# An interleave of two arrays: whole-tile stores in longer rows, three shared load buffers and a shrinking tail

## The chip, the cores and the metric

The kernel runs on one core of a Trainium2 chip. The metric is the device time of one execution in microseconds. The profile is one execution with the hardware profiler on; its span is a little shorter than the device time, since it runs from the first to the last recorded instruction.

## What is computed

Two float32 arrays of 32 x 256 x 1024 (33.55 MB each) are interleaved along the last axis into one of 32 x 256 x 2048:

```python
result = np.zeros((batch, seq, dim * 2), dtype=np.float32)
result[..., 0::2] = x
result[..., 1::2] = y
```

There is no arithmetic. 67.1 MB are read and 67.1 MB are written.

## The kernel before

Since the interleave doesn't care about rows, the kernel treats x, y and out as flat lists: element i of x goes to place 2i, element i of y to place 2i + 1. The lists are cut into 8 pieces of 128 x 8192 elements. In a piece, each of the 128 partitions holds one stretch of 8192 neighbouring elements, so one load moves 128 rows of 32 KB.

One pass of the loop (L50) does this:

- SP issues the load of x (L56) and of y (L57) into `xtile` and `ytile`. Each has its own pool with two buffers of 32 KB per partition.
- VectorE handles the piece in two halves (L60). For each half it copies 4096 columns of x into the even places of `otile` (L70), and 4096 columns of y into the odd places (L71). `otile` comes from a pool with two buffers of 32 KB per partition.
- ACT issues the store of each half (L72): 128 rows of 32 KB.

So there are two queues, one for loads (q1 in the profile, issued by SP) and one for stores (q10, issued by ACT). Each engine issues in the order of the program. A load waits until the copies have read the buffer that it overwrites (two passes ago); the first copy of a half waits until the store that last used its `otile` buffer (two halves ago) has landed; a store waits for both copies.

Ahead of the loop, a store of 16 rows of 512 bytes of zeros goes out on ACT's queue (L47); the first real store overwrites its place in the output. After the program is built, the first load is moved ahead of the opening barrier (L86 to L104), so that it starts early. The change leaves both as they are, but for the distance between the zero rows, which follows the width of a tile.

Of the kernel before, what the change touches and what calls it, by code (L numbers as in the profile page):

```python
# [2 lines left out]

# [4 lines left out]


@with_exitstack
def _interleave(
    ctx: ExitStack,
    tc: tile.TileContext,
    x: bass.AP,
    y: bass.AP,
    out: bass.AP,
):
    nc = tc.nc
    P = 128  # L20

    total = 1
    for s in x.shape:
        total *= s

    WL = 8192
    WS = 4096

    xf = x.rearrange("b s d -> (b s d)")
    yf = y.rearrange("b s d -> (b s d)")  # L30
    of = out.rearrange("b s d -> (b s d)")

    fp32 = mybir.dt.float32

    xpool = ctx.enter_context(tc.tile_pool(name="xp", bufs=2))
    ypool = ctx.enter_context(tc.tile_pool(name="yp", bufs=2))
    opool = ctx.enter_context(tc.tile_pool(name="op", bufs=2))

    lwidths = [WL] * (total // P // WL)
    assert sum(lwidths) == total // P  # L40


    wpool = ctx.enter_context(tc.tile_pool(name="wp", bufs=1))
    zero = wpool.tile([16, 128], fp32, name="zero")
    nc.vector.memset(zero, 0.0)  # L45
    first = dataclasses.replace(of, offset=0, ap=[[2 * WL, 16], [1, 128]])
    nc.scalar.dma_start(out=first, in_=zero)  # L47

    start = 0
    for lw in lwidths:  # L50
        xtile = xpool.tile([P, WL], fp32, name="xtile")[:, :lw]
        ytile = ypool.tile([P, WL], fp32, name="ytile")[:, :lw]

        xs = dataclasses.replace(xf, offset=start, ap=[[lw, P], [1, lw]])
        ys = dataclasses.replace(yf, offset=start, ap=[[lw, P], [1, lw]])
        nc.sync.dma_start(out=xtile, in_=xs)  # L56
        nc.sync.dma_start(out=ytile, in_=ys)  # L57

        soff = 0
        while soff < lw:  # L60
            width = min(WS, lw - soff)
            otile = opool.tile([P, 2 * WS], fp32, name="otile")[:, : 2 * width]
            os_ = dataclasses.replace(
                of,
                offset=2 * start + 2 * soff,
                ap=[[2 * lw, P], [1, 2 * width]],
            )
            xsub = xtile[:, soff : soff + width]
            ysub = ytile[:, soff : soff + width]
            nc.vector.tensor_copy(out=otile[:, 0::2], in_=xsub)  # L70
            nc.vector.tensor_copy(out=otile[:, 1::2], in_=ysub)  # L71
            nc.scalar.dma_start(out=os_, in_=otile)  # L72
            soff += width

        start += P * lw
    assert start == total


def kernel(tc, x, y, out):
    nc = tc.nc  # L80
    _interleave(tc, x, y, out)
    tc.close()
    tc.compile()  # L83


    blocks = nc.main_func.blocks  # L86
    opening = blocks[0].instructions
    at, moved = next(
        (b, i)
        for b in blocks[1:]  # L90
        for i in b.instructions
        if i.engine == mybir.EngineType.SP and i.opcode == "DMACopy"
    )
    assert not moved.sync_info.on_wait
    body = at.instructions
    body.remove(moved)
    gate = next(
        n
        for n, i in enumerate(opening)
        if i.engine == mybir.EngineType.SP and i.opcode == "Drain"  # L100
    )
    opening.insert(gate, moved)
    at.instructions = body
    blocks[0].instructions = opening  # L104


# [1 line left out]
_INS = ['x', 'y']  # L108
_OUTS = [((32, 256, 2048), 'float32')]


# [23 lines left out]
```

## Time and profile before

| | before |
|---|---|
| device time, median of 3 runs | 316.41 us (315.72 to 316.87) |
| span of the profiled execution | 313.8 us |
| VectorE busy | 72.8 us, 23% |
| DMA | 134.23 MB, mean 428 GB/s |
| copies of 128 x 4096 | 32, of 2.29 us each |
| loads | 16, of 4096 KB, rows of 32 KB |
| stores | 16, of 4096 KB, rows of 32 KB |

The page gives the busy time of each engine, the span in 40 slices, and the share of 16 DMA engines that each queue's packets took. A packet is here one row of a transfer, or one completion signal of a few bytes. A transfer of 128 rows gives 8 rows to each of the 16 DMA engines. A transfer has "landed" when all 16 have signalled.

### The profile page before, as it was taken

Reading aid. Unit: us, or ns where it says so; the run is one execution under the profiler, and the core shown is the slowest. Engines: PE = TensorE matmul, PEld = TensorE weight load, DVE = VectorE, ACT = ScalarE, POOL = GpSimd, SP = SyncE. Lnnn points to the kernel's source line nnn. Section 1 sums busy time; section 2 is a strip of 40 time slices with the busy share of each in tenths; the row PEclk is TensorE's granted clock in tenths of the full one; section 3 lists DMA queues with packets and bytes.
Section 4 is the critical chain, followed back from the end, with each engine's and each line's share of the span. In section 5 each row is a group of like instructions: output and inputs, shape, how many; then the busy total and the mean of one; then the engine's idle time right before and its main releaser. Section 6 shows DMA issues by size and latency. Waiting matters only on the chain.

```text
span 313.8 us, 152 instructions
## 1 busy us (share of the span) xinstructions
DVE 72.8 (23%) x33; POOL 0.2 (0%) x4
## 2 busy tenths in 40 slices
DVE  0433002231032410325003150130501305023500
POOL 0000000000000000000000000000000000000000
DMA  8999999999999999999999999999999999999997
GB/s 339 464 405 397 468 401 464 405 464 405 464 405 464 405 459 409 451 418 451 418 434 434 430 439 426 443 413 455 401 468 401 468 401 468 401 468 401 464 405 334
DMA packets 4640, 134.23 MB, mean 428 GB/s; under 512 B 528, under 2 KB 544, under 8 KB 544
## 3 DMA queue, kind: packets, MB, share of 16 engines
q1 hardware_dynamic: 2304, 67.11, 49.9%
q10 hardware_dynamic: 2336, 67.12, 49.5%
HBM read 67.11 MB, written 67.12 MB: 428 GB/s over the span
## 4 chain that ended last, share of the span: by engine, by line
DMA 83%; DVE 11%; DVEq 1%; issue 0%
DMA out_dram<-otile 76%; DMA ytile<-in_y_dram 7%; DVE otile L71 6%; DVE otile L70 5%; DVEq L83 1%; DVEq L70 0%
## 5 line engine op out<-in xcount | busy, mean ns | idle before, releaser
L70 DVE COPY otile<-xtile 128x4096 f32<-128x4096 f32 x16 | 36.6, 2295 | 184.9 <-DMA out_dram<-otile 173.7
L71 DVE COPY otile<-ytile 128x4096 f32<-128x4096 f32 x16 | 36.6, 2292 | 39.8 <-DMA ytile<-in_y_dram 39.8
L45 DVE MEMSET zero<- 16x128 f32 x1 | 0.2, 165 | 0.9 <-PEq L119 0.9
L119 POOL MEMSET const-bfloat16-1.0<- 128x1 bf16 x1 | 0.1, 102 | 0.0
L119 POOL MEMSET const-uint8-127<- 128x1 uint8 x1 | 0.1, 102 | 0.0
L119 POOL MEMSET const-float32-0.0<- 128x1 f32 x1 | 0.1, 99 | 0.2 <-issue 0.2
L119 POOL MEMSET const-float32-1.0<- 128x1 f32 x1 | 0.1, 99 | 0.0
## 6 DMA issues: line engine op xcount, KB each, us to landing
out_dram<-otile ACTq DMA_DIRECT2D x16, 4096.0 KB, 29.1
xtile<-in_x_dram SPq DMA_DIRECT2D x8, 4096.0 KB, 43.6
ytile<-in_y_dram SPq DMA_DIRECT2D x8, 4096.0 KB, 60.7
out_dram<-zero ACTq DMA_DIRECT2D x1, 8.0 KB, 6.3
```

Source lines behind the costliest of these rows:

```text
L45: nc.vector.memset(zero, 0.0)
L70: nc.vector.tensor_copy(out=otile[:, 0::2], in_=xsub)
L71: nc.vector.tensor_copy(out=otile[:, 1::2], in_=ysub)
L83: tc.compile()
L119: nc = _bacc.Bacc("TRN2", target_bir_lowering=False, num_devices=1)
```

## The change

The widths are now a list: eight tiles of 7296 columns (28.5 KiB rows in x and y), then tiles of 4096, 2048 and 1024. Their sum is the same 65536 columns per partition. A tile is no longer stored in halves: VectorE copies the whole of x and the whole of y into an `otile` of twice the width, and one store writes rows of 57 KiB. As this takes more room per `otile` buffer (57 KiB, still two), x and y share one pool of three load buffers instead of two each. The shrinking tiles at the end are there so that the last copies and the last store are short.

```diff
-    WL = 8192
-    WS = 4096
+    WIDTHS = [7296] * 8 + [4096, 2048, 1024]
+    WMAX = max(WIDTHS)
...
-    xpool = ctx.enter_context(tc.tile_pool(name="xp", bufs=2))
-    ypool = ctx.enter_context(tc.tile_pool(name="yp", bufs=2))
+    lpool = ctx.enter_context(tc.tile_pool(name="lp", bufs=3))
     opool = ctx.enter_context(tc.tile_pool(name="op", bufs=2))
...
+    for w in WIDTHS:
+        tiles = []
+        for src in (xf, yf):
+            t = lpool.tile([P, WMAX], fp32, name="ltile")[:, :w]
+            rows = dataclasses.replace(src, offset=start, ap=[[w, P], [1, w]])
+            nc.sync.dma_start(out=t, in_=rows)
+            tiles.append(t)
+        otile = opool.tile([P, 2 * WMAX], fp32, name="otile")[:, : 2 * w]
+        for i, t in enumerate(tiles):
+            nc.vector.tensor_copy(out=otile[:, i::2], in_=t)
+        rows = dataclasses.replace(of, offset=2 * start, ap=[[2 * w, P], [1, 2 * w]])
+        nc.scalar.dma_start(out=rows, in_=otile)
+        start += P * w
```

There are now 22 loads, 22 copies and 11 stores.

More of the change, by code (lines that the diff above doesn't have):

```diff
@@ L24, in _interleave @@
         total *= s
-    WL = 8192
-    WS = 4096
+    assert P * sum(WIDTHS) == total
     xf = x.rearrange("b s d -> (b s d)")
@@ L33, in _interleave @@
     fp32 = mybir.dt.float32
-    xpool = ctx.enter_context(tc.tile_pool(name="xp", bufs=2))
-    ypool = ctx.enter_context(tc.tile_pool(name="yp", bufs=2))
+    wpool = ctx.enter_context(tc.tile_pool(name="wp", bufs=1))
+    lpool = ctx.enter_context(tc.tile_pool(name="lp", bufs=3))
     opool = ctx.enter_context(tc.tile_pool(name="op", bufs=2))
-    lwidths = [WL] * (total // P // WL)
-    assert sum(lwidths) == total // P
-    wpool = ctx.enter_context(tc.tile_pool(name="wp", bufs=1))
     zero = wpool.tile([16, 128], fp32, name="zero")
@@ L45, in _interleave @@
     nc.vector.memset(zero, 0.0)
-    first = dataclasses.replace(of, offset=0, ap=[[2 * WL, 16], [1, 128]])
+    first = dataclasses.replace(of, offset=0, ap=[[2 * WIDTHS[0], 16], [1, 128]])
     nc.scalar.dma_start(out=first, in_=zero)
     start = 0
[L50 to L75, printed above, removed]
@@ L76, in _interleave @@
-    assert start == total
+    for w in WIDTHS:
[11 more added lines that the diff above has]
+        start += P * w
```

## The prediction

> **What bounds the kernel now.** I read the slices of the page first, then the DMA queues, then stretches of the trace, and the waits and the chain last, because the first two already say that one resource is full.
>
> ```profile
> DMA  8999999999999999999999999999999999999997
> ...
> q1 hardware_dynamic: 2304, 67.11, 49.9%
> q10 hardware_dynamic: 2336, 67.12, 49.5%
> ```
>
> The two shares are of 16 engines over 313.8 us, and they add to 99.4%: q1 carries the loads, q10 the stores, and the DMA engines have next to no idle time between the first slice and the last. VectorE, at 23%, cannot be the bound. Each queue moved 2048 rows of 32 KB (16 transfers of 128 rows). A store row takes 0.495 x 16 x 313.8 / 2048 = 1.213 us. A load row averages 1.223 us; by the packet records the excess is in two places, the first row of each engine (1.47 to 2.27 us) and one row of each at 26 to 29 us, as the first big store comes in (1.69 to 1.88 us); all others take 1.21 to 1.23.
>
> Next, stretches of one loop pass each (start:end, length, VectorE busy, GpSimd busy, clock, DMA share, GB/s):
>
> ```profile
> 67.44:106.16 38.72, 9.09 (x4) 0.00 (x0) 1.00 1.00 433
> 106.16:144.89 38.73, 9.09 (x4) 0.00 (x0) 1.00 1.00 433
> 144.89:183.61 38.72, 9.09 (x4) 0.00 (x0) 1.00 1.00 433
> ```
>
> A pass moves 16.78 MB in 38.72 us at DMA share 1.00, and it repeats. Eight passes are 309.8 us of the 313.8. The other 4 us are 0.99 us ahead of the first row, some 1.3 us of slow first rows, and the end (last row ends at 312.70, landing 313.06, span 313.8).
>
> The waits and the chain must be read beside this:
>
> ```profile
> DVE otile L70 <- DMA out_dram<-otile: 173.7, 14, 21.6
> DVE otile L71 <- DMA ytile<-in_y_dram: 39.8, 8, 5.2
> ...
> DMA 83%; DVE 11%; DVEq 1%; issue 0%
> ```
>
> VectorE waits for stores to leave their buffers, and the chain counts 11% of copies between stores. It would be wrong to call these 11% a gain: the stretches above, which hold those copies, have the DMA at 1.00. While one buffer is copied, the other store is still running. The end shows it too:
>
> ```profile
> 293.80 2.30 DVE otile L70
> 296.09 2.20 DVEq L83
> ```
>
> The last pair of copies runs to 298.3 us, but the store before it lands only at 303.4, so the last store goes straight in behind it.
>
> **What the Trainium skill says.** "DMA: Bandwidth & Descriptors", section "Where 436 GB/s comes from", puts the ceiling of the 16 ports at 435.2 GB/s. The trace agrees: 433 in every pass. There is no rate left to win. The same page, "Queues, rings and completion order", says that an engine takes turns between its queues packet by packet. In the trace between 29.1 and 48 us, with both queues full, the rows are shared like this:
>
> ```profile
> q1 hardware_dynamic: 144, 4.19, 51.4%
> q10 hardware_dynamic: 142, 4.13, 50.6%
> ```
>
> That is one row for one row (each count includes 16 completions). Before, where all rows are equal, turns by row and turns by bytes look alike; I take turns by row. "Why small descriptors are slow" states a fixed cost per packet. The trace prices it: the 16 rows of 512 bytes of the zero store took 3.6% of 16 engines in a stretch of 0.75 us, so 27 ns each, against 1213 ns for 32768 bytes. The line through both has 8.2 ns per row and 0.0368 ns per byte.
>
> **The change, part by part.** I call the eight large tiles 0 to 7 and the small ones A (4096), B (2048), C (1024).
>
> *Rows.* Bytes stay. Rows per engine go from 256 to 22 x 8 + 11 x 8 = 264. DMA work: 8 x 8.2 ns = 0.07 us more, 310.6 instead of 310.5. Stores have 40 rows fewer, loads 48 more. A large load row takes 29184 x 0.0368 + 8 = 1.08 us (a transfer 8.65), a large store row 2.15 (17.2). For A, B, C a load takes 4.88, 2.47, 1.27 and a store 9.70, 4.88, 2.47. Assuming that the straight line reaches 57 KB is a choice; it is beyond the sizes seen.
>
> *Copies.* 32 become 22. From 2.29 us for 4096 columns: 4.09 us for 7296, then 2.29, 1.15, 0.57. The elements are the same, so VectorE stays near 73 us in all, hidden as long as the DMA has rows.
>
> *Start.* Three loads instead of four are issued at once. They last 1 + 0.7 + 3 x 8.65 = 27.7 us. The fourth needs only the copy of x of tile 0, over at about 1.7 + 8.65 + 0.4 + 4.1 = 14.9 us. Nothing is lost, and the 0.99 us and the slow rows stay.
>
> *Middle.* A load now waits for the copy of the load three before; SP issues in order, so every later load is queued behind it. A copy of x waits for the store two tiles before. Suppose store t and load y of tile t+1 start together: by row they alternate for 8 x (1.08 + 2.15) = 25.9 us and end together. Then x of t+2 runs alone, 8.65 us; in sum 34.5 us, which is the DMA work of a tile. Meanwhile y of t+1 has to land (0.4 us, as after the last row of all, or up to one store row more), be copied (4.09) and its store has to reach its first row. That last step is unknown: the first load of all took 0.99 us from issue to row, in empty rings; the zero store took 4.2 and the first big store (issued at 24.3) up to 4.8, both behind load rows. So 5.5 to 11.7 us. Loads to move in this time: x of t+2 and, behind it, y of t+2, issued as soon as x of t+1 is copied, over 20 us earlier; 17.3 us together. So no gap. Three load buffers are enough, and the middle costs nothing either way.
>
> *End.* Load rows xA to yC are 48 per engine. Between 9 and 15 are through when store 7 starts; 16 more alternate with the rows of stores 7 and A. So after the last row of A, yB has 1 to 7 rows left, and then only the 16 rows of C, 2.5 us. In this time yB has to land (0.4), be copied (1.15; x of B is copied earlier, its buffer being free since store 7) and store B has to reach its first row (1.0 to 4.6). The DMA stands idle for 2.55 - 2.54 = 0.0 us at the low end, 3.6 at the high end. I take 1.3 for that last step, because the ring has no long rows in it then (a row of C is 0.16 us), and so 0.3 us. Store B lasts 4.88 us, which hides landing and copy of C (0.4 + 0.57). The last landing costs what it did.
>
> Sum: +0.07 + 0.3, so 316.41 + 0.4 = **316.8 us**, no change that can be told.
>
> **Rivals.** *The end is slower.* If the 4.2 to 4.8 us of a store's start are a fixed delay and not load rows ahead of it, B starts 3.6 us late: 316.4 + 0.1 + 3.6 = 320.1 us. For it: both starts on that queue show about the same delay. Against it: in both the engine then had a row of 1.2 to 2.2 us in hand[...], which explains the same. Delays in between give 317.4 to 319. Chance 0.25 in all, 0.08 of it for the full delay.
>
> *Fewer rows in the stores pay.* If store rows over 32 KB cost less than the line says, or the slow first rows are fewer, the most to be had is 40 x 8.2 ns = 0.33 us with the 1.3 us of slow rows, 1.6 us in all, with nothing lost at the end: 314.8, or 315.2 if most of it comes. For it: those are the only losses that the trace shows outside the passes. Against: nothing in the change touches the first load. Chance 0.18.
>
> *The loads starve the stores.* If the three buffers left the DMA idle during one copy of each large tile, 8 x 4.09 = 33 us come on top: 349. Against it stand the 17.3 us of queued loads. Chance 0.02.
>
> **How the numbers follow.** No change: 0.55, with 315.5 to 317.3. Slower by over 0.3%: 0.25 + 0.02 = 0.27. Faster: 0.18. The range leaves out the full delay and starving (0.10) above, with the worst of the partial delays, and the larger part of the faster case's lower end (0.08) below: 315.2 to 318.5.
>
> **What will show it.** In the profile after: passes of about 34.5 us at DMA share 1.00 and 433 GB/s; both queues' shares adding to 99% or more; mean row times near 1.08 and 2.15 us; waits of y copies for loads, which cost nothing. In the last 15 us the slices show a dip ahead of store B: under 0.5 us confirms, 2 us and over is the first rival. A pass under 34.3 us would mean that long rows are cheaper; one clearly over 34.6, or DMA shares below 0.97 in the middle, that turns, buffers or row cost are not as I think.

## The result and the profile after

The changed kernel is slower: 334.35 us (331.64 to 339.1) against 316.49 us, a ratio of 1.0546 with a 95% interval of 1.0482 to 1.061. The forecast was no change, 316.8 us, with a range up to 318.5. Ratios and their intervals, here and below, leave out executions more than 1.5% above the fastest of the same kernel (here the one of 339.1 us), so a ratio can differ a little from that of the medians. The profiled execution has a span of 334.0 us, 20.2 us more than before.

First the slices and queues of the page after:

```profile
DMA  8999999999999999999999998999999996999948
GB/s 350 433 444 388 426 370 391 398 454 426 391 412 444 444 395 430 416 423 447 381 402 419 416 468 381 419 409 416 416 400 413 427 389 264 398 410 459 390 165 345
...
q1 hardware_dynamic: 3168, 67.11, 48.9%
q10 hardware_dynamic: 1616, 67.12, 47.9%
```

The bytes are those of before. The two shares add to 96.8% of a longer span, so the DMA engines were busy for 323 us instead of 312. Two dips in the GB/s row (264 and 165) stand near the end. So there are two losses: rows that take longer, and idle engines in the last 60 us.

The stretches from one store's issue to the next show the first (start:end, length, VectorE, GpSimd, clock, DMA share, GB/s):

```profile
63.56:102.75 39.19, 7.92 (x2) 0.00 (x0) 1.00 1.01 419
102.75:138.30 35.55, 7.92 (x2) 0.00 (x0) 1.00 1.00 422
138.30:173.44 35.14, 7.92 (x2) 0.00 (x0) 1.00 1.01 415
...
208.77:248.51 39.74, 7.92 (x2) 0.00 (x0) 1.00 1.00 416
248.51:283.46 34.95, 7.92 (x2) 0.00 (x0) 1.00 0.90 375
```

The DMA share is 1.00, just as in the passes of before, but at 415 to 422 GB/s instead of 433. A busy engine is no longer an engine at its rate. The six passes from 63.56 to 283.46 us take 36.7 us on average; 34.5 were forecast. In the last of them, with a share of 0.90, engines already stand idle.

That the rows themselves are longer can be read from the queue lines, cut to 63.56 to 248.51 us:

```profile
q1 hardware_dynamic: 1544, 40.04, 52.0%
q10 hardware_dynamic: 720, 37.36, 48.2%
```

37.36 MB are 640 store rows of 58368 bytes: 0.482 x 16 x 184.95 / 640 = 2.23 us each, where the straight line of the prediction has 2.15. 1372 load rows take 1.12 us, where it has 1.08. By the packet records of the whole execution most rows are on the line: the median of these load rows is 1.081 us, of the 57 KB store rows 2.154 us. But 188 of 2048 load rows and 133 of 1024 store rows are over it by more than 0.1 us, by up to 1.6.

The second loss shows in short stretches of the end:

```profile
280.00:284.00 4.00, 3.43 (x1) 0.00 (x0) 1.00 0.29 123
...
320.00:324.00 4.00, 0.87 (x1) 0.00 (x0) 1.00 0.10 40
```

A DMA share of 0.29 and 0.10: little moves, and it is load rows that a few engines are late with. In the first, the load of y of tile 7 has landed late, at 279.4 us, and its copy, to 283.4, holds back both the next load (its buffer) and the next store. In the second, all wait for y of the tile of 2048 to land, at 323.1 us. The waits of VectorE and of SP's own queue name it:

```profile
DVE otile L54 <- DMA ltile<-in_y_dram: 174.4, 11, 24.4
DVE otile L54 <- DMA ltile<-in_x_dram: 79.0, 10, 14.2
...
SPq L50 <- DMA ltile<-in_y_dram: 162.9, 9, 24.0
```

Before, copies of x waited for stores; now copies wait for loads. That alone is no sign of a loss: e1 below, which loses next to nothing, waits for loads too (120.4 us for x, 117.0 for y). What differs is that some single waits are long, up to 24.4 us against 13.4 there. The chain of waits has turned round in the same way:

```profile
DMA 70%; another core or an unknown queue 18%; DVE 10%; issue 0%; DVEq 0%
DMA ltile<-in_x_dram 54%; DMA ltile<-in_y_dram 16%; DVE otile L54 10%; DVEq L54 0%
```

Stores are not in it. The 18% of "unknown queue" on one core alone are the waits of 19.6 us for the last completion of a load of y, as in the chain's pieces:

```profile
255.89 3.96 DVE otile L54
259.85 19.59 another core or an unknown queue
279.44 0.02 issue
```

That load's first DMA engine had signalled at 248.1 us, the last at 279.4: a spread of 31 us between engines that each move 8 equal rows. Before, the widest spread in any transfer was 0.6 us. The engines have fallen out of step.

Three figures from the packet and completion records sum this up, and I use them for all runs below. **Excess** is the time of all rows of 4 KB or more over the line (8.2 ns + 0.0368 ns per byte), divided by 16. **Idle** is the time between the first and the last row in which an engine moves no row, as a mean of the 16. **Spread** is the time from the first to the last of the 16 completions of a transfer, median and largest. All three are of the one profiled execution, which for e2 (341.66 us), e10 (324.96 us) and e12 (320.16 us) was that kernel's longest. The records don't name a row's engine; where I write "us per engine", it is a sum over all rows divided by 16.

| kernel | load row / store row | ratio to before | excess us | idle us | spread us |
|---|---|---|---|---|---|
| before | 32 / 32 KB | 1 | 1.3 | 0 | 0.4, 0.6 |
| after | 28.5 / 57 KB | 1.0546 | 12.3 | 8.9 | 6.3, 31.3 |
| e1, stores split | 28.5 / 28.5 | 1.0042 | 1.9 | 0 | 1.7, 2.2 |
| e2, no shrinking tail | 28.5 / 57 | 1.0645 | 15.7 | 11.7 | 8.3, 30.3 |
| e3 | 16 / 32 | 1.0261 | 5.6 | 4.2 | 2.2, 13.8 |
| e6 | 32 / 16 | 1.0093 | 3.8 | 0 | 0.8, 5.2 |
| e7, large tiles split | 28.5 / 28.5, then 1 to 2 | 1.0066 | 1.9 | 0.1 | 1.9, 2.2 |
| e8, small tiles split | 28.5 / 57, then equal | 1.0533 | 9.6 | 6.3 | 5.4, 28.3 |
| e9, four load buffers | 25 / 50 | 1.0585 | 13.1 | 5.7 | 5.4, 25.4 |
| e10, y on a third queue | 25 / 50 | 1.0166 | 4.5 | 5.8 | 3.7, 15.9 |
| e11 | 40 / 40 | 1.0047 | 1.8 | 0.3 | 1.8, 2.2 |
| e12, three stores held | 32 / 32 | 1.0031 | 2.6 | 3.0 | 3.6, 9.8 |
| e13 | 15.5 / 31 | 1.0252 | 6.3 | 1.8 | 2.9, 12.4 |
| c1, copies left out | 48 / 48 | 1.0071 | 3.1 | 3.1 | 3.2, 13.4 |
| c2, copies left out | 24 / 48 | 1.0368 | 9.7 | 3.2 | 3.4, 13.0 |
| c3, copies left out | 24 / 24 | 1.0030 | 1.7 | 0 | 0.6, 1.6 |

The 20.2 us of the span are thus accounted for: 11.0 us of longer rows and 8.9 us of idle engines. Of the excess of 12.3 us, 7.4 lie in load rows and 4.9 in store rows; before, all of it lay in load rows.

### The profile page after: what moved, and what is told of

It reads as the page before. It is cut to its first block, busy times and chain, and to the rows that moved or that the text cites. A ratio compares the mean times of both kernels' runs of the same rounds, so it can differ in the third digit from the quotient of the medians.

```text
span 334.0 us, 140 instructions
## 1 busy us (share of the span) xinstructions
DVE 72.0 (22%) x23; POOL 0.2 (0%) x4
## 3 DMA queue, kind: packets, MB, share of 16 engines
q10 hardware_dynamic: 1616, 67.12, 47.9%
HBM read 67.11 MB, written 67.12 MB: 402 GB/s over the span
## 4 chain that ended last, share of the span: by engine, by line
DMA 70%; another core or an unknown queue 18%; DVE 10%; issue 0%; DVEq 0%
DMA ltile<-in_x_dram 54%; DMA ltile<-in_y_dram 16%; DVE otile L54 10%; DVEq L54 0%
## 5 line engine op out<-in xcount | busy, mean ns | idle before, releaser
L54 DVE COPY otile<-ltile 128x7296 f32<-128x7296 f32 (+3 forms) x22 | 71.8, 3264 | 253.5 <-DMA ltile<-in_y_dram 174.4
```

The costliest lines, as they stand in the source:

```text
L54: nc.vector.tensor_copy(out=otile[:, i::2], in_=t)
```

## The experiments

### Undo the row length alone (e1)

Everything of the change stays, tiles, buffers, tail; each whole-tile store is issued as two transfers of half rows.

```diff
-        nc.scalar.dma_start(out=rows, in_=otile)
+        for h in range(2):
+            rows = dataclasses.replace(
+                of, offset=2 * start + h * w, ap=[[2 * w, P], [1, w]]
+            )
+            nc.scalar.dma_start(out=rows, in_=otile[:, h * w : (h + 1) * w])
```

> The changed kernel, but each tile's store goes out as two transfers of 28.5 KB rows, one behind the other; tiles, widths, load buffers, copies and tail are those of the change. Theory 1 (turns): the DMA engines take turns row for row, so stores with rows twice as long as the loads' get two thirds of the bytes, run dry once per tile, and each new start costs a slow row on each engine, puts the engines out of step and makes every later wait one for the slowest engine. Then equal rows bring nearly all back: 316 to 319 us, one slow spot at the first store as before. Theory 2 (rows over 32 KB are slow in themselves): also 316 to 319. Theory 3 (the shrinking tail): no less than 325. Theory 4 (row pitches of 28.5 KB that are no power of two): about 334. Theory 5 (three shared load buffers): about 334.

317.1 us, ratio 1.0042 (1.0027 to 1.0057). The passes between issues are back at the rate of before:

```profile
52.05:86.55 34.50, 7.92 (x2) 0.00 (x0) 1.00 1.00 433
86.55:121.07 34.52, 7.92 (x2) 0.00 (x0) 1.00 1.00 433
121.07:155.58 34.51, 7.92 (x2) 0.00 (x0) 1.00 1.00 433
```

So 28.5 KB pitches (the distance between rows), three shared load buffers, whole-tile copies and the shrinking tail cost next to nothing as long as the stores' rows are short; the loss needs the 57 KB rows. Whether it is their length or that they are longer than the loads', e1 can't tell; c1 below does. The 1.2 us that stay over before are partly known: 96 rows per engine more than before, at 8.2 ns each, are 0.8 us.

### The tail (e2, e7, e8)

```diff
-    WIDTHS = [7296] * 8 + [4096, 2048, 1024]
+    WIDTHS = [7296] * 8 + [7168]
```

> The changed kernel with [7296] * 8 + [7168] for widths: no shrinking tiles. Theory 3 (the tail's small tiles lose the time): clearly faster than the change, 320 to 326 us. Theories 1, 2, 4, 5 (the loss is made by the large tiles, and the tail only shows it): the middle loses its 10 us as before, and the last large tile adds its copy (4 us) and its store's start with nothing beside it: 332 to 340 us.

336.69 us, 1.0645 (1.0609 to 1.0681): without the small tiles it is no better, so they don't make the loss.

Then the split of e1 for a part of the tiles, `n = 2 if w == WMAX else 1` transfers per store in e7, `n = 2 if w < WMAX else 1` in e8.

> The changed kernel, where only the eight large tiles are stored by two transfers of 28.5 KB rows; the tiles of 4096, 2048 and 1024 keep whole-tile stores with rows twice their loads'. Theory 1 with the idle time of the end made by engines that were put out of step in the large tiles: 316.5 to 319 us. Theory 3' (the idle 9 us at the end are made by the small tiles' own ratio): 324 us or more.

> The opposite part alone: the large tiles keep 57 KB rows in the stores, the tiles of 4096, 2048 and 1024 are stored by two transfers with rows equal to their loads'. Theory 1: still 328 to 336 us, since slow rows and engines out of step come from the large tiles. Theory 3': 323 to 327 us, the 9 us of idle time at the end being gone.

e7 has 317.82 us (1.0035 to 1.0096), e8 336.27 us (1.0452 to 1.0615). The idle 9 us of the end go away when the *large* tiles are mended, though the small ones keep store rows of twice their load rows; and they stay, 6.3 us, when only the small ones are. I read it so: the engines come into the tail out of step, and with few rows left and three load buffers the fast ones run out of work while a few slow ones finish.

### Only the ratio, with nothing else of the change (e3, e13)

The kernel before with pieces of 4096 columns, each stored whole: 16 KB loads, 32 KB stores.

```diff
-    WL = 8192
+    WL = 4096
     WS = 4096
```

> The kernel before with pieces of 4096 columns: loads in 16 KB rows, whole-piece stores in 32 KB rows, all powers of two, no row over 32 KB, two buffers each for x and y, no shrinking tail. Only the ratio of store row to load row (2 to 1) is that of the change. Theory 1 (turns): the store queue runs dry in each of the 16 passes, each start costs 0.4 to 0.7 us per engine and the engines drift apart: 324 to 335 us. Theory 2 (long rows), theory 4 (pitch) and theory 5 (three buffers): none applies, 316 to 318 us.

323.79 us, 1.0261 (1.0233 to 1.029). No row is over 32 KB, every pitch is a power of two and x and y have two buffers each, and still 2.6% are lost, 7.9 us, of which by the line 1.05 us are 128 more load rows per engine. So unequal rows do it without anything else of the change. The store queue was empty at nine of the 15 later store issues, not at each as expected. The ratio does less here than in the change, and e13 asks whether the pitch is the difference (`WL = WS = 3968`, widths `[3968] * 16 + [2048]`).

> As the run with 16 KB loads and 32 KB whole-piece stores, but with pieces of 3968 columns (15.5 KB loads, 31 KB stores, a last piece of 2048): the ratio and nearly the length stay, and the pitch is no power of two any more. If the pitch makes the loss of the unequal rows larger: 330 us or more, towards the 334 of the change. If it is the length of the rows: like the run with 16 and 32 KB (323.8 us), 322 to 327 us.

324.14 us, 1.0252 (1.0229 to 1.0274). The pitch makes no difference here. At the same ratio the kernels with store rows of 48 to 57 KB lose more (1.0368 to 1.0585); but they differ in buffers and tiles too, so that it is the length is not shown.

### The queues by themselves (c1, c2, c3)

These leave out the interleave and with it VectorE's copies: a tile is loaded and sent from the same buffer. c2 and c3 differ in the stores' rows alone. c1 has longer load rows, and also moves all of x before y.

```diff
+    for w in [OW // 2] * 10 + [4096]:                       # c2, OW = 12288
+        t = lpool.tile([P, OW], fp32, name="ltile")[:, : 2 * w]
+        for h, src in enumerate((xf, yf)):
+            rows = dataclasses.replace(src, offset=start, ap=[[w, P], [1, w]])
+            nc.sync.dma_start(out=t[:, h * w : (h + 1) * w], in_=rows)
+        rows = dataclasses.replace(of, offset=2 * start, ap=[[2 * w, P], [1, 2 * w]])
+        nc.scalar.dma_start(out=rows, in_=t)
```

> Leaves out the interleave: tiles are loaded in 48 KB rows and stored from the same buffer in 48 KB rows (four buffers), with no VectorE copies, so the same bytes cross with rows equal on both queues, all over 32 KB and no power of two. Theory 1 (turns): equal rows, both queues stay full: 314 to 318 us, rows on the straight line of 0.0368 ns per byte, 1.82 us. Theory 2 (long rows are slow): rows of both queues well over 1.82 us on average, 322 us or more. Theory 4 (pitch): the same as theory 2.

> Leaves out the interleave: two loads of 24 KB rows fill the halves of a tile, one store sends it in 48 KB rows (four buffers), with no VectorE copies. Against the copy kernel with 48 KB rows on both queues (318.5 us) only the rows of the loads are halved. Theory 1 (turns; a matter of the queues alone): the store queue runs dry between tiles, slow rows at each store's start, landings spread over many us: 324 to 335 us. Rival (VectorE's copies, or the waits through them, are needed for the loss): 317 to 320 us.

> Leaves out the interleave, as the other two copy kernels do: loads of 24 KB rows fill the halves of a tile, and two stores of 24 KB rows send it; no VectorE copies. Against the copy kernel with 24 KB loads and 48 KB stores (327.5 us) only the rows of the stores are halved. Equal rows (theory 1): one slow spot at the first store, 316 to 319.5 us. If the tiles' pitch or the tile's four buffers made the loss there: 325 us or more.

c1 318.52 us (1.0045 to 1.0098), c2 327.53 us (1.0329 to 1.0407), c3 316.91 us (1.0021 to 1.0039). The median row of 48 KB takes 1.815 us in c1, on the line: **long rows are not slow in themselves**. With the loads' rows halved (c2) the time is 9 us longer; halving the stores' too, and nothing else (c3), brings 10.6 us back. VectorE's copies and their waits aren't needed for the loss.

### The turns (e9, e10, e6)

If the loss comes from row-for-row turns between two queues, a third queue should mend it at unchanged row lengths: a round is then two load rows and one store row, the same bytes each way. The change's widths leave too little room for a fourth load buffer, so both kernels have `[6400] * 10 + [1536]` and four; e10 alone has

```diff
-            nc.sync.dma_start(out=t, in_=rows)
+            queue = nc.gpsimd if src is yf else nc.sync
+            queue.dma_start(out=t, in_=rows)
```

> Control for the next run: the changed kernel with widths [6400] * 10 + [1536] and four load buffers (25 KB load rows, 50 KB store rows), still one queue for loads and one for stores. Theory 1 (turns): another load buffer does not help, the store queue runs dry in each of the ten large tiles: 325 to 340 us, 8 us or more of slow rows. Rival (theory 5, it is the three load buffers): 316 to 319 us.

> The same, but y is loaded through a third queue, GpSimd's. Rows keep their lengths (25 KB loads, 50 KB stores); only the turns change: with three queues a round is two load rows and one store row, so 50 KB each way, and neither side should run dry. Theory 1: slow rows go but for the first store's, 316 to 319 us. Rival (unequal row lengths on the DMA engines are slow in themselves, whatever the turns): like the control, 325 us or more. What could spoil it: the third queue's own cost[...], of which no run here shows anything.

e9: 334.53 us (1.0546 to 1.0623), so a fourth buffer doesn't help. e10: 322.3 us (1.0108 to 1.0225). The queues of e10 over the whole span:

```profile
q10 hardware_dynamic: 1616, 67.12, 48.3%
q0 software_dynamic: 1584, 33.56, 24.7%
q1 hardware_dynamic: 1584, 33.56, 24.6%
```

The loads' 33.56 MB twice and the stores' 67.12 MB take 1:1:2 of the time, and at every store's issue from the second on a store row was still running on at least 3 engines; in e9 the queue was empty at the issue of each of the ten large stores, and each of these starts after the first came with 19 to 36 slow load rows (over the line by more than 0.05 us, within 6 us of the issue). Excess falls from 13.1 to 4.5 us, in load rows from 8.9 to 3.7 and in store rows from 4.2 to 0.9. So the third queue takes away two thirds of the loss of e9, as turns by row would have it. Not all: spread and idle time stay above those of equal rows, and 322.3 misses the 316 to 319 expected. What of the rest belongs to unequal lengths and what to GpSimd's queue, no run tells.

e6 turns the ratio round (`WS = 2048`, four store buffers).

> The kernel before with pieces stored in quarters: loads in 32 KB rows, stores in 16 KB rows, four store buffers of 16 KB. The ratio is turned round, so by row-for-row turns the loads take two thirds of the bytes, run ahead until their buffers are full, and it is the load queue that runs dry and starts again in each pass; the store queue stays full. Work by the line: 128 store rows per engine more, +1.05 us. Theory 1a (only the start of a store in an empty store queue costs slow rows): 317 to 318 us, one slow spot at the first store. Theory 1b (any queue with the longer rows runs dry and its restarts cost the same): 322 us or more, slow rows at each restart of the loads.

319.22 us, 1.0093 (1.0075 to 1.0111), between the two expectations. 1.05 of the 3.0 us are the extra rows; excess is 3.8 us. Here the load queue ran dry, five times, and its new starts came with at most 19 slow load rows, 0.33 us per engine. Long load rows beside short store rows cost far less than the reverse.

### Is it the running dry alone? (e12)

The change's store queue runs dry once per large tile; before's, once it has started, does not. Two views of the change between 70 and 82 us and between 94 and 106 us show it:

```profile
q10 hardware_dynamic: 62, 3.62, 71.5%
q1 hardware_dynamic: 61, 1.61, 31.0%
```

```profile
q1 hardware_dynamic: 192, 5.02, 99.7%
q10 hardware_dynamic: 5, 0.12, 2.3%
```

First 62 store rows to 55 load rows (the count of q1 has 6 completions), near one for one, so 3.62 MB of stores against 1.61 MB of loads; later loads alone. At 6 of the 7 starts of stores 1 to 7 no store row was running, and at each of these 15 to 23 load rows were slow in the sense given for e9, 0.4 to 0.85 us per engine. The seven starts together are 4.4 us, less than half of the 11.0. e12 makes the kernel before run dry three times with equal rows, by holding back halves 3, 7 and 11:

```diff
+            if 2 * start // (P * lw) + soff // WS in (3, 7, 11):
+                for _ in range(3):
+                    nc.vector.tensor_copy(out=otile, in_=otile)
             nc.scalar.dma_start(out=os_, in_=otile)
```

> The kernel before with the stores of halves 3, 7 and 11 held back: VectorE copies that store buffer onto itself three times (128 x 8192, with no change of content) before the store may go. As the store ahead of it lands in the meantime, the store queue runs dry three times for 5 to 10 us, while enough loads are queued to keep the DMA engines busy. All rows stay 32 KB on both queues. Theory 1a (it is the running dry: each start of the store queue beside running loads costs one slow row on each engine, whatever the rows' lengths): three further slow spots of 0.4 to 1 us per engine beside the first store's, 317.5 to 320 us. Theory 1b (a start costs only where the rows on the two queues are unequal, or the slow rows come from the mixture of lengths): one slow spot as before, 316 to 317 us.

316.52 us, 1.0031 (1.0011 to 1.0051). The store queue did run dry; from 89 to 99 us only this moved:

```profile
q1 hardware_dynamic: 144, 4.19, 97.1%
```

Yet at the three restarts 1, 0 and 5 load rows were slow, 0.10 us per engine at most. Theory 1a, a fixed price on every start, falls; 1b stands: of the starts seen, the dear ones stand beside unequal rows (the very first store's apart). Running dry isn't quite free either: the execution that was profiled took 320.16 us, the longest of that kernel's 20 (from 315.6), and in it the spread grew to 9.8 us.

### A version built on the finding (e11)

Equal rows, as long as memory allows: `WL = 10240`, `WS = 5120`, widths `[10240] * 6 + [4096]`, three load buffers shared.

> A version built on theory 1: rows as long as the memory allows with equal rows on both queues. Pieces of 10240 columns and a last one of 4096, stored in halves; loads and stores in 40 KB rows, three load buffers shared by x and y, two store buffers. Rows per engine fall from 256 to 224, work by the line 0.26 us less than before. Theory 1: 315 to 317.5 us, no difference from before that can be told, one slow spot. Theories 4 and 5 (pitch that is no power of two, three buffers): 325 us or more.

317.06 us, 1.0047 (1.0029 to 1.0066). Equal rows of 40 KB keep the DMA on the line, but 32 rows fewer per engine bring nothing that can be seen. No kernel tried is faster than before.

## Why the prediction was wrong

**What bounds the kernel: right.** The DMA engines are the bound in both kernels, and no kernel tried was faster than before. e11 has 32 rows fewer per engine, so the second rival, that fewer rows pay, did not come true either.

**Row-for-row turns: right**, and the structure of a tile that was worked out from it, alternation and then loads alone, is in the two views above. No gap in the middle: right, the DMA share is 1.00 until 248.5 us. The rival of starving buffers, an idle DMA during a copy of each large tile, does not occur there; e1 with the same three buffers has no idle time, and e9 with four is no faster.

**The step that failed is the middle's "costs nothing either way".** It took a busy DMA for one at 433 GB/s: rows were priced by a line drawn through rows of before, in which both queues always had equal rows. I had called this line's reach a choice because 57 KB was beyond it. The length was not the trouble (c1); the mixture was. The row term, priced at 0.07 us, measured 11.0 us, most of it in the middle. The prediction's own sign for this, a pass clearly over 34.6 us, is what the profile shows. The trace of before held one hint, and the prediction named it without using it: as the first store came in, there were 20 slow load rows, 0.63 us per engine (one of 1.69 to 1.88 us for each engine, as the prediction says, and four more of 1.33 to 1.58 us). The walk of the middle showed that this kernel's store queue starts anew in each tile, so the case of that spot coming back with each of seven further large stores should have been priced: 7 x 0.63 = 4.4 us, 321 us, slower and outside the range. That would have hit what the seven starts cost, but by luck: in e12, where rows are equal, three new starts cost 0.10 us each at most. And it would have left out the larger part of the loss.

**The end failed by its landing time.** It took 0.4 us from last row to landing, or one store row more, from a kernel whose engines march in step. With engines apart the landing of a load is that of its slowest engine, 6.3 us after the fastest by the median. That made 8.9 us of idle time out of 0.3. Its sum for a late start of the store, 5.5 to 11.7 us, comes to 11.4 at the top by the terms that it names; nothing hangs on it. The narrower dispute there was decided as forecast: the store of the tile B, issued at 324.39 us into an empty queue, had its first row 0.84 us later, so the rival of a fixed delay of 4.2 us and more is wrong. (Beside running load rows the large stores had their first row 2.5 to 4.6 us after the issue.)

**The first rival had the right side and the wrong cause.** The end does lose more than forecast, but e8 shows that mending the tail's own rows leaves the loss.

What stays open: why an engine's row is stretched when a long store row joins short load rows, why later store rows run over the line, and why the reverse ratio costs less. The records hold a row's start and length, not what it waited for. The runs show only when these things come and go.

## What to carry to other kernels

Where a load queue and a store queue keep the DMA engines full, as here, give both rows of the same length; a wide tile can still be stored by two transfers of half rows, at 1.0042 of the time before against 1.0546. Don't read a DMA share of 1.00 as full rate: put the GB/s, or a row's mean time, beside it. When a change makes one queue run dry in turn, look for what the trace shows at the one place where that queue starts, and give the case that it comes back once per turn a price and a chance. Then try it: here the new starts cost 4.4 us with unequal rows and next to nothing with equal ones.

## What was not expected of the hardware

- Rows twice as long in the stores as in the loads cost 2.6% at 16 and 32 KB (0.3% of it for the number of rows) and 5.5% at 28.5 and 57 KB. The reverse ratio (32 and 16 KB) costs 0.9%, a third of it for the number of rows.
- The 16 DMA engines can drift apart by up to 31 us within one transfer. With equal rows and full queues its largest value is 0.6 to 2.2 us (before, e1, e11, c3). c1 has more, 13.4 us, in the load of its last narrow tile, whose 16 KB rows meet store rows of 48 KB.
- Rows of 48 KB with equal rows on both queues run on the same line, 8.2 ns and 0.0368 ns per byte, as rows of 0.5 to 32 KB: 1.815 us.
